# 128x128 turns in a two-layer hybrid decoder: one transposing matmul a block, or four 64x64 products on TensorE's four quarters

## The chip, the cores and the metric

The kernel runs on one core of one Trainium2 chip. The metric is the device time of one execution in microseconds (us). All matmuls run on TensorE, whose results land in PSUM banks of 128 partitions x 512 fp32 columns; ScalarE and VectorE copy them out.

## The reference

Two layers of a causal decoder trunk on x of shape (1, 256, 1024) in fp32, each with two half-step feed-forward blocks around four parallel mixers:

```python
x = x + 0.5 * swiglu(rmsnorm(x), w_gate, w_up, w_down)      # 1024 -> 2816 -> 1024
h = rmsnorm(x); parts = split(h @ w_in)                      # 1024 -> 12288
y = [hgrn2(q, f, i, g), s5(u), conformer_conv(a, b), dilated_attention(q, k, v)]   # each 512 wide
x = x + (sum(sigmoid(gate_k) * (y_k @ w_branch_k))) @ w_out
x = x + 0.5 * swiglu(rmsnorm(x), ...)
```

A last rmsnorm ends it. Attention has 12 heads of 128 (3 groups of dilation 1, 4 and 16) with partial rotary positions; the 256 tokens are two blocks of 128.

## The kernel before

The work is bound to weights that are read once. A stream (`Stream`) loads fp32 weights from HBM, ScalarE rounds them to a high part (`whi`) and VectorE takes the low part (`wlo`), both as fp32r; each product of activations and weights is three fp32r matmuls (`mm3`: high x high, high x low, low x high). The activations are split in the same way by `split`: one ScalarE copy and one VectorE subtraction, from PSUM or SBUF.

TensorE runs the products of one stage behind the other: `cols_tok` makes rows of tokens (512 columns a matmul), `cols_feat` and `rows_feat` make rows of features (256 columns, all tokens). The mixers' own work (rope and attention, HGRN2, S5, the convolution, the tables of S5) is written as generators in a list `side`; after each piece of a stage `tick` steps them, as far as `room` allows. It decides by clocks that a planner keeps for each engine (`Paced`), with costs such as `pe_cost` for TensorE. `finish` steps a job to its end without regard to the clocks, where its result is needed. PSUM has four accumulation banks and four others (`mx`), which side jobs reserve with `grab` and `drop` from the count `free`.

Between the stages tensors are turned, from tokens on partitions to features on partitions or back, in blocks of 128x128. Such a turn is `T.transpose(bank[:, ...], block, ident)`: the block is the stationary operand and the identity matrix the moving one. Four blocks fill one bank, which is then copied out:

- `norm_turn` (L913): the normed activations `xn` of one token block, 8 blocks in two banks `xT`, then split into `hTh` and `hTl`. `norm.turn(0)` stands among the last matmuls of the stage before; `norm.turn(1)` stands in the next stage between its matmuls for the first and the second 128 tokens.
- `turn` in `ffn` (L986): the first 512 columns of the gated activations, 4 blocks for each token block, `gT`.
- `s5_tables` (L632): tables `b4` (4 blocks in each of 4 banks a layer) and `s5c`.
- `rope_turn` (L1369): queries and keys, up to 4 heads for each token block, `rt`, copied out by heads.
- `attend` (L1416): the weights `scores` after the exponential, 3 blocks for the first 128 queries and 6 (in two banks one behind the other) for the others, `pTb`; copied to `pT`, which is the stationary operand of the product with the values (`apv`).
- `hgrn`, `conv` and the end of `attend`: the mixers' outputs, `yaT`, `cT` and `cB`, `ydT`, 4 blocks a bank.

The S5 mixer makes its small products as 64x64x64 matmuls on the four quarters of TensorE: rows 0 to 63 or 64 to 127 of the operands by partitions 0 to 63 or 64 to 127 of the result (names `s5k`, `yk`, `w`, `y`). `yk` goes through the quarters in the order (0, 0), (1, 1), (0, 1), (1, 0) of operand half and result half.

Of the kernel before, what the change touches and what calls it, by code (L numbers as in the profile page):

```python
# [75 lines left out]
def size(ap):  # L76
    return math.prod(ap.shape[1:])
# [29 lines left out]
def pe_cost(name, args):  # L107
    if name == "transpose":
        return 0.11
    n = size(args[2])  # L110
    return max(0.107, n / 2370 * (1 if args[2].dtype == FR else 4))
# [77 lines left out]
def trunk(ctx, tc, x_in, positions, ffn1_norm, ffn1_w_gate, ffn1_w_up, ffn1_w_down, mix_norm, w_in,  # L189
# [31 lines left out]
    def tiny(shape, name, bufs=4):  # L221
        return sb.tile(shape, F32, tag=name, name=name, bufs=bufs)

# [138 lines left out]
    free = [3]  # L362
# [269 lines left out]
    def s5_tables(l):  # L632
# [51 lines left out]
        for half in range(2):  # L684
            hs = slice(4 * half, 4 * half + 4)
            bv = [bb[:, k].rearrange("p (a h) c -> p a h c", a=2)[:, :, hs, None, :] for k in range(2)]
            qv = [pq[:, k].rearrange("p i (a h) -> p a h i", a=2)[:, :, hs, :, None] for k in range(2)]
            for k, op in ((0, ALU.subtract), (1, ALU.add)):
# [7 lines left out]
                yield  # L696
                b = mx_bank(f"b4{half}{k}")
                ov = o.rearrange("p h a i c -> p h (a i c)")
                for h in range(4):
                    T.transpose(b[:, h * P:(h + 1) * P], ov[:, h], ident)  # L700
                S.activation(B4[half][:, :, k, :], b.rearrange("p (h s) -> p h s", h=4), AF.Copy)
                yield GO
# [9 lines left out]
        for k in range(2):  # L712
            b = mx_bank(f"s5c{k}")
            for a in range(4):
                T.transpose(b[:, a * P:(a + 1) * P], craw[k][:, a].rearrange("p g s -> p (g s)"), ident)
            bv = b.rearrange("p (j g c) -> p j g c", g=2, c=16)
            for g in range(2):
                S.activation(ct[64 * g:64 * g + 64, k], bv[64 * g:64 * g + 64, :, g, :], AF.Copy)
            yield
# [193 lines left out]
    def norm_turn(t, xn, n, hT):  # L913
        for b in range(2):
            bank = tr_bank(f"xT{n}_{t}{b}")
            for i in range(4):
                f = 4 * b + i
                T.transpose(bank[:, i * P:(i + 1) * P], xn[:, f * P:(f + 1) * P], ident)
            bv = bank.rearrange("p (k f) -> p k f", k=4)
            split(hT[0][b][:, :, t * P:(t + 1) * P], hT[1][b][:, :, t * P:(t + 1) * P], bv)  # L920
# [46 lines left out]
    def ffn(norm, tail):  # L967
# [3 lines left out]
        for c, (c0, n) in enumerate(FFC):  # L971
# [5 lines left out]
            if c == 0:  # L977
# [4 lines left out]
                def ev_up(t, bank, gh=gh, gl=gl, sg=sg):  # L982
                    V.tensor_tensor(sg[t], bank, sg[t], op=ALU.mult)
                    g = sg[t]

                    def turn():  # L986
                        yield
                        b = tr_bank(f"gT{t}")
                        for i in range(4):
                            T.transpose(b[:, i * P:(i + 1) * P], g[:, i * P:(i + 1) * P], ident)  # L990
                        split(gh[:, :, t * P:(t + 1) * P], gl[:, :, t * P:(t + 1) * P],
                              b.rearrange("p (k f) -> p k f", k=4))
                    start(turn())
# [69 lines left out]
    def mixers(l, norm, tail, g_tab):  # L1063
# [7 lines left out]
        def pair(name):  # L1071
            return H([P, 4, 256], name + "h", FR), H([P, 4, 256], name + "l", FR)


        def hgrn():
# [103 lines left out]
            yT[0] = pair("yA")  # L1179
            for t in range(2):  # L1180
# [15 lines left out]
                y = H2([P, 512], "ya")  # L1196
# [6 lines left out]
                b2 = tr_bank(f"yaT{t}")  # L1203
                for i in range(4):
                    T.transpose(b2[:, i * P:(i + 1) * P], y[:, i * P:(i + 1) * P], ident)
                split(yT[0][0][:, :, t * P:(t + 1) * P], yT[0][1][:, :, t * P:(t + 1) * P],
                      b2.rearrange("p (k f) -> p k f", k=4))
                yield
# [107 lines left out]
        def conv():  # L1316
# [15 lines left out]
            for t in range(2):  # L1332
                yield from grab()
                b = tr_bank(f"cT{t}")
                for fb in range(4):
                    T.transpose(b[:, fb * P:(fb + 1) * P], a[:, fb, t * P:(t + 1) * P], ident)
                st = tiny([P, 6], "bst", 2)
                mv = tiny([P, 4], "bmv", 2)
                V.bn_stats(st, b)
# [5 lines left out]
                V.tensor_scalar(xc[t], b, mv[:, 0:1], mv[:, 3:4], op0=ALU.subtract, op1=ALU.mult)  # L1345
                drop()
                yield
            yT[2] = pair("yC")
            for half in range(2):
                b = tr_bank(f"cB{half}")  # L1350
                for i in range(2):
                    fb = 2 * half + i
                    for t in range(2):
                        T.transpose(b[:, i * 256 + t * P:i * 256 + (t + 1) * P], xc[t][:, fb * P:(fb + 1) * P], ident)
                y = H2([P, 2, 256], "yc")
                for i in range(2):
# [3 lines left out]
                    S.activation(y[:, i, :], b[:, i * 256:(i + 1) * 256], AF.Silu, bias=vcol[:, cb_:cb_ + 1],  # L1360
                                 scale=vcol[:, cg:cg + 1])
                split(yT[2][0][:, 2 * half:2 * half + 2, :], yT[2][1][:, 2 * half:2 * half + 2, :], y)
                yield
# [5 lines left out]
        def rope_turn(raw, pieces, name):  # L1369
# [14 lines left out]
            for t in range(2):  # L1384
                b = tr_bank(f"{name}{t}")
                for i in range(n):
                    T.transpose(b[:, i * P:(i + 1) * P], rv[:, t, i, :], ident)
# [290 lines left out]
```

## Time and profile before

| | |
|---|---|
| median of 3 runs | 1568.28 us (1562.89 to 1569.6) |
| profiled execution | 1563.96 us, span 1562.3 us |
| TensorE matmuls | busy 1548.3 us (99%), 11419 instructions |
| weight loads of TensorE | busy 1413.7 us (90%) |
| VectorE | busy 1104.7 us (71%) |
| ScalarE | busy 843.4 us (54%) |
| DMA | weight queue 51.9% of 16 engines' span, HBM 179 GB/s |
| granted TensorE clock | 0.997 of full speed |

Busy time counts an engine as busy while an instruction of it is in flight. Matmuls are pipelined: one lasts 218 to 400 ns, and the next starts long before it has ended, so what a matmul costs is the distance from its start to the next one's start. In the tables of rows PE is TensorE's matmul side, PEld its weight loads, DVE is VectorE, ACT ScalarE. L72 is the line of the planner's wrapper, through which nearly every instruction is issued, so groups are told apart by the names of their tiles.

### The profile page before, as it was taken

What the parts mean: (1) busy time and instruction counts of PE and PEld (TensorE: products, weight loads), DVE (VectorE), ACT (ScalarE), POOL (GpSimd) and SP (SyncE); (2) the same over time, 40 slices, a digit from 0 to 9 for tenths busy, and PEclk for the clock granted to TensorE, in tenths of its full rate; (3) what the DMA queues carried; (4) which work ended last, traced back from release to release, by engine and by line L of the source; (5) the groups of instructions that cost most, each with busy time, mean ns of one, the idle gap of its engine ahead of it and who ended that gap; (6) DMA issues with size and microseconds to landing.
All of it is one profiled execution on the core that took longest, in us unless ns stands there. A gap on an engine that the chain in (4) does not pass through costs nothing.

```text
span 1562.3 us, 27640 instructions
## 1 busy us (share of the span) xinstructions
PE 1548.3 (99%) x11419; PEld 1413.7 (90%) x11419; DVE 1104.7 (71%) x1767; ACT 843.4 (54%) x1212; POOL 28.0 (2%) x75
## 2 busy tenths in 40 slices
PE   9999999999999999999999999999999999999998
PEld 7999888889899998999889988988899999989986
DVE  6787676966878866555497766568869887665553
ACT  5644465666565465444354553656665565654442
POOL 2000000000000000000000000000000000000000
PEclk9999999999999999999999999999999999999999
DMA  7566556453544556556556564665345544645561
GB/s 274 189 194 218 189 182 202 153 172 109 162 163 162 177 183 220 189 183 214 183 176 197 188 216 160 205 197 167 129 137 170 180 163 163 227 164 191 196 217 58
DMA packets 179376, 281.94 MB, mean 180 GB/s; under 512 B 26703, under 2 KB 82065, under 8 KB 179250
## 3 DMA queue, kind: packets, MB, share of 16 engines
q1 hardware_dynamic: 154096, 270.03, 51.9%
q10 hardware_dynamic: 24834, 9.97, 2.6%
q8 instruction: 89, 1.46, 0.4%
q14 instruction: 37, 0.30, 0.1%
q0 software_dynamic: 320, 0.18, 0.0%
HBM read 277.01 MB, written 3.15 MB: 179 GB/s over the span
## 4 chain that ended last, share of the span: by engine, by line
PE 96%; ACT 1%; DVE 1%; issue 1%; DMA 1%; POOL 0%; ACTq 0%; SPq 0%; POOLq 0%; DVEq 0%
PE down L72 15%; PE gate_h L72 13%; PE up_h L72 13%; PE att_t L72 12%; PE pgt_h L72 11%; PE br L72 6%; PE gate_t L72 3%; PE up_t L72 3%; PE po_t L72 3%; PE pi_t L72 1%; PE pu_h L72 1%; PE pb_h L72 1%; PE pg_t L72 1%; PE pa_h L72 1%; PE glu L72 1%; PE pq_h L72 1%
## 5 line engine op out<-in xcount | busy, mean ns | idle before, releaser
L72 DVE TENSOR_TENSOR wlo<-raw,whi 128x1024 fp32r<-128x1024 f32 x512 | 614.4, 1220 | 185.7 <-ACT whi L72 88.4
L72 ACT ACTIVATE whi<-raw 128x1024 fp32r<-128x1024 f32 x512 | 526.6, 1055 | 157.6 <-PE down L72 90.1
L72 PE MATMUL gate_h<-hTh,whi 128*128 128x256 f32 x576 | 160.1, 278 | 0.0
L72 PE MATMUL up_h<-hTh,whi 128*128 128x256 f32 x576 | 159.3, 277 | 0.0
L72 PE MATMUL gate_h<-hTh,wlo 128*128 128x256 f32 x576 | 159.1, 276 | 0.0
L72 PE MATMUL gate_h<-hTl,whi 128*128 128x256 f32 x576 | 159.1, 276 | 0.0
L72 PE MATMUL up_h<-hTh,wlo 128*128 128x256 f32 x576 | 159.0, 276 | 0.0
L72 PE MATMUL up_h<-hTl,whi 128*128 128x256 f32 x576 | 159.0, 276 | 0.0
L72 PE MATMUL pgt_h<-hTh,whi 128*128 128x256 f32 x512 | 144.9, 283 | 0.0
L72 PE MATMUL pgt_h<-hTl,whi 128*128 128x256 f32 x512 | 141.9, 277 | 0.0
L72 PE MATMUL pgt_h<-hTh,wlo 128*128 128x256 f32 x512 | 141.9, 277 | 0.0
L72 PE MATMUL down<-whi,gl 128*128 128x512 f32 x352 | 138.5, 393 | 0.0
L72 PE MATMUL down<-whi,gh 128*128 128x512 f32 x352 | 138.1, 392 | 0.0
L72 PE MATMUL down<-wlo,gh 128*128 128x512 f32 x352 | 138.0, 392 | 0.0
L72 PE MATMUL att_t<-whi,hTh 128*128 128x512 f32 x288 | 118.6, 412 | 0.0
L72 PE MATMUL att_t<-whi,hTl 128*128 128x512 f32 x288 | 114.3, 397 | 0.0
L72 PE MATMUL att_t<-wlo,hTh 128*128 128x512 f32 x288 | 113.6, 395 | 0.0
L72 PEld LDWEIGHTS gate_h<-hTl,whi 128*128 128x128 f32 x576 | 108.2, 188 | 0.0
L72 PEld LDWEIGHTS gate_h<-hTh,whi 128*128 128x128 f32 x576 | 108.2, 188 | 0.1
L72 PEld LDWEIGHTS up_h<-hTl,whi 128*128 128x128 f32 x576 | 108.1, 188 | 0.0
L72 PEld LDWEIGHTS up_h<-hTh,whi 128*128 128x128 f32 x576 | 108.1, 188 | 0.0
L72 PEld LDWEIGHTS gate_h<-hTh,wlo 128*128 128x128 f32 x576 | 108.1, 188 | 0.0
(391 smaller groups left out, 3344.8 us busy)
## 6 DMA issues: line engine op xcount, KB each, us to landing
raw<-in_w_in_dram SPq DMA_DIRECT2D x60, 1024.0 KB, 5.2
raw<-in_ffn_w_up_dram SPq DMA_DIRECT2D x44, 1024.0 KB, 5.3
raw<-in_ffn_w_down_dram SPq DMA_DIRECT2D x44, 1024.0 KB, 4.9
raw<-in_ffn_w_gate_dram SPq DMA_DIRECT2D x42, 1024.0 KB, 5.1
raw<-in_w_in_dram SPq DMA_DIRECT2D x72, 512.0 KB, 4.6
raw<-in_w_branch_dram SPq DMA_DIRECT2D x16, 1024.0 KB, 5.0
raw<-in_w_out_dram SPq DMA_DIRECT2D x8, 1024.0 KB, 5.1
raw<-in_s_w_glu_dram SPq DMA_DIRECT2D x16, 256.0 KB, 3.8
```

Of the source, the lines that this page charges most:

```text
L72: return f(*args, **kw)
```

## The change

Each turn becomes four plain matmuls of 64x64 blocks with the matching 64x64 corner of the identity matrix, one on each quarter of TensorE. A helper `turn` takes a list of up to eight 128x128 blocks and fills two banks: bank `r` holds, for each block, the 64 columns that come from its rows 64r to 64r + 63. What was two groups of four blocks, one for each token block or each half, becomes one call of eight where both are there: `gT`, `rt`, `yaT` and `ydT` (by `turn_out`), `b4`, `s5c`, `cB`; attention turns its six blocks at once before the product with the values. The copies out of PSUM read a bank with 64 tokens of each block, and write them to their place (`half_rows`); for `norm_turn` these are four copies of 256 columns in place of two of 512. Side jobs reserve two banks for a turn, and `free` goes from 3 to 4. The planner's `pe_cost` has a price of 0.036 us for a matmul whose stationary operand is 64x64, which holds for the S5 products too (0.108 us before).

```diff
--- before.py
+++ after.py
@@ -108,6 +108,8 @@
     if name == "transpose":
         return 0.11
     n = size(args[2])
+    if args[1].shape[0] == 64 and size(args[1]) == 64:
+        return 0.036
     return max(0.107, n / 2370 * (1 if args[2].dtype == FR else 4))
 
 
@@ -220,6 +222,20 @@
 
     def tiny(shape, name, bufs=4):
         return sb.tile(shape, F32, tag=name, name=name, bufs=bufs)
+
+    def turn(name, blocks):
+
+
+        banks = [mx_bank(f"{name}{r}") for r in range(2)]
+        for i, src in enumerate(blocks):
+            for r, c in ((0, 0), (1, 1), (0, 1), (1, 0)):
+                rs, cs = slice(64 * r, 64 * r + 64), slice(64 * c, 64 * c + 64)
+                T.matmul(banks[r][cs, 64 * i:64 * i + 64], src[rs, cs], ident[rs, rs], start=True, stop=True)
+        return banks
+
+    def half_rows(ap, r, pattern):
+
+        return ap.rearrange(pattern + " (t r q) -> " + pattern + " t r q", r=2, q=64)[..., r, :]
 
     def split(hi, lo, src, eng_hi=None):
         S.activation(hi, src, AF.Copy)
@@ -359,7 +375,7 @@
             for j in list(side):
                 step(j)
 
-    free = [3]
+    free = [4]
 
     def grab(n=1):
 
...
@@ -693,13 +710,13 @@
                     V.tensor_tensor(u2[:, :, a], bv[1 - k][:, a].to_broadcast([P, 4, 4, 16]),
                                     qv[1][:, a].to_broadcast([P, 4, 4, 16]), op=ALU.mult)
                 V.tensor_tensor(o, u1, u2, op=op)
-                yield
-                b = mx_bank(f"b4{half}{k}")
-                ov = o.rearrange("p h a i c -> p h (a i c)")
-                for h in range(4):
-                    T.transpose(b[:, h * P:(h + 1) * P], ov[:, h], ident)
-                S.activation(B4[half][:, :, k, :], b.rearrange("p (h s) -> p h s", h=4), AF.Copy)
-                yield GO
+                ov.append(o.rearrange("p h a i c -> p h (a i c)"))
+                yield GO if k == 0 else None
+            banks = turn(f"b4{half}", [o[:, h] for o in ov for h in range(4)])
+            for r in range(2):
+                S.activation(B4[half][:, :, :, 64 * r:64 * r + 64].rearrange("p h k q -> p k h q"),
+                             banks[r].rearrange("p (k h q) -> p k h q", k=2, h=4), AF.Copy)
+            yield GO
         dx = H2([16, 2, 4, 16], "dx")
         V.tensor_copy(dx, draw[:, :, None, :].to_broadcast([16, 2, 4, 16]))
         yield
@@ -709,14 +726,14 @@
         V.tensor_copy(dcol, b[:, 0:16])
 
         ct = H2([P, 2, 16, 16], "ct")
-        for k in range(2):
-            b = mx_bank(f"s5c{k}")
-            for a in range(4):
-                T.transpose(b[:, a * P:(a + 1) * P], craw[k][:, a].rearrange("p g s -> p (g s)"), ident)
-            bv = b.rearrange("p (j g c) -> p j g c", g=2, c=16)
+        banks = turn("s5c", [craw[k][:, a].rearrange("p g s -> p (g s)") for k in range(2) for a in range(4)])
+        for r in range(2):
+            bv = banks[r].rearrange("p (a j g c) -> p a j g c", j=2, g=2, c=16)
+            cv = ct.rearrange("p k (a r j) c -> p (k a) r j c", r=2, j=2)
             for g in range(2):
-                S.activation(ct[64 * g:64 * g + 64, k], bv[64 * g:64 * g + 64, :, g, :], AF.Copy)
-            yield
+                gs = slice(64 * g, 64 * g + 64)
+                S.activation(cv[gs, :, r], bv[gs, :, :, g, :], AF.Copy)
+        yield
         for half in range(2):
             hs = slice(8 * half, 8 * half + 8)
             cv = [ct[:, k, hs, None, :].to_broadcast([P, 8, 4, 16]) for k in range(2)]
@@ -911,13 +928,12 @@
     norm_no = [0]
 
     def norm_turn(t, xn, n, hT):
+        banks = turn(f"xT{n}_{t}", [xn[:, f * P:(f + 1) * P] for f in range(8)])
         for b in range(2):
-            bank = tr_bank(f"xT{n}_{t}{b}")
-            for i in range(4):
-                f = 4 * b + i
-                T.transpose(bank[:, i * P:(i + 1) * P], xn[:, f * P:(f + 1) * P], ident)
-            bv = bank.rearrange("p (k f) -> p k f", k=4)
-            split(hT[0][b][:, :, t * P:(t + 1) * P], hT[1][b][:, :, t * P:(t + 1) * P], bv)
+            for r in range(2):
+                ts = slice(t * P + 64 * r, t * P + 64 * r + 64)
+                split(hT[0][b][:, :, ts], hT[1][b][:, :, ts],
+                      banks[r][:, 256 * b:256 * b + 256].rearrange("p (k q) -> p k q", k=4))
 
     class Norm:
 
@@ -981,16 +997,15 @@
 
                 def ev_up(t, bank, gh=gh, gl=gl, sg=sg):
                     V.tensor_tensor(sg[t], bank, sg[t], op=ALU.mult)
-                    g = sg[t]
-
-                    def turn():
+
+                    def turn_g():
                         yield
-                        b = tr_bank(f"gT{t}")
-                        for i in range(4):
-                            T.transpose(b[:, i * P:(i + 1) * P], g[:, i * P:(i + 1) * P], ident)
-                        split(gh[:, :, t * P:(t + 1) * P], gl[:, :, t * P:(t + 1) * P],
-                              b.rearrange("p (k f) -> p k f", k=4))
-                    start(turn())
+                        banks = turn("gT", [sg[t][:, i * P:(i + 1) * P] for t in range(2) for i in range(4)])
+                        for r in range(2):
+                            split(half_rows(gh, r, "p i"), half_rows(gl, r, "p i"),
+                                  banks[r].rearrange("p (t i q) -> p i t q", t=2, i=4))
+                    if t == 1:
+                        start(turn_g())
                 cols_tok(hT, ev_gate, "gate0", outer=True, between=lambda: norm.turn(1), at=3 if norm.n == 0 else 4,
                          mid=norm.n == 0)
                 cols_tok(hT, ev_up, "up0")
@@ -1071,6 +1086,17 @@
         def pair(name):
             return H([P, 4, 256], name + "h", FR), H([P, 4, 256], name + "l", FR)
 
+        def turn_out(b, y):
+
+            yT[b] = pair("y" + "ABCD"[b])
+            yield from grab(2)
+            banks = turn(f"y{b}T", [y[t][:, i * P:(i + 1) * P] for t in range(2) for i in range(4)])
+            for r in range(2):
+                split(half_rows(yT[b][0], r, "p i"), half_rows(yT[b][1], r, "p i"),
+                      banks[r].rearrange("p (t i q) -> p i t q", t=2, i=4))
+            drop(2)
+            yield
+
 
         def hgrn():
             qT, kT, Pm = m["qT"], m["kT"], m["lf"]
...
@@ -1193,19 +1219,14 @@
                 V.tensor_scalar(ss[:, 0:4], ss[:, 0:4], EPS, None, op0=ALU.add)
                 G.tensor_tensor(ss[:, 4:8], ss[:, 0:4], neghalf.to_broadcast([P, 4]), op=ALU.pow)
                 yield
-                y = H2([P, 512], "ya")
+                ys[t] = y = H2([P, 512], "ya")
                 for h in range(4):
                     hs = slice(h * P, (h + 1) * P)
                     V.scalar_tensor_tensor(y[:, hs], b[:, hs], ss[:, 4 + h:5 + h], sgn[:, t, hs], op0=ALU.mult,
                                            op1=ALU.mult)
                 drop()
                 yield
-                b2 = tr_bank(f"yaT{t}")
-                for i in range(4):
-                    T.transpose(b2[:, i * P:(i + 1) * P], y[:, i * P:(i + 1) * P], ident)
-                split(yT[0][0][:, :, t * P:(t + 1) * P], yT[0][1][:, :, t * P:(t + 1) * P],
-                      b2.rearrange("p (k f) -> p k f", k=4))
-                yield
+            yield from turn_out(0, ys)
 
 
         def s5():
@@ -1330,36 +1351,38 @@
             yield
             xc = {}
             for t in range(2):
-                yield from grab()
-                b = tr_bank(f"cT{t}")
-                for fb in range(4):
-                    T.transpose(b[:, fb * P:(fb + 1) * P], a[:, fb, t * P:(t + 1) * P], ident)
-                st = tiny([P, 6], "bst", 2)
+                yield from grab(2)
+                banks = turn(f"cT{t}", [a[:, fb, t * P:(t + 1) * P] for fb in range(4)])
+                st = tiny([P, 2, 6], "bst", 2)
                 mv = tiny([P, 4], "bmv", 2)
-                V.bn_stats(st, b)
+                for r in range(2):
+                    V.bn_stats(st[:, r], banks[r][:, 0:256])
                 V.bn_aggr(mv[:, 0:2], st)
                 V.tensor_scalar(mv[:, 2:3], mv[:, 1:2], EPS, None, op0=ALU.add)
                 G.tensor_tensor(mv[:, 3:4], mv[:, 2:3], neghalf, op=ALU.pow)
                 yield
                 xc[t] = H2([P, 512], f"xc{t}")
-                V.tensor_scalar(xc[t], b, mv[:, 0:1], mv[:, 3:4], op0=ALU.subtract, op1=ALU.mult)
-                drop()
+                for r in range(2):
+                    V.tensor_scalar(half_rows(xc[t], r, "p"), banks[r][:, 0:256].rearrange("p (b q) -> p b q", b=4),
+                                    mv[:, 0:1], mv[:, 3:4], op0=ALU.subtract, op1=ALU.mult)
+                drop(2)
                 yield
             yT[2] = pair("yC")
+            yield from grab(2)
+            banks = turn("cB", [xc[t][:, fb * P:(fb + 1) * P] for fb in range(4) for t in range(2)])
             for half in range(2):
-                b = tr_bank(f"cB{half}")
-                for i in range(2):
-                    fb = 2 * half + i
-                    for t in range(2):
-                        T.transpose(b[:, i * 256 + t * P:i * 256 + (t + 1) * P], xc[t][:, fb * P:(fb + 1) * P], ident)
                 y = H2([P, 2, 256], "yc")
                 for i in range(2):
                     fb = 2 * half + i
                     cg = col["lg"] + 4 * l + fb
                     cb_ = col["lbn"] + 4 * l + fb
-                    S.activation(y[:, i, :], b[:, i * 256:(i + 1) * 256], AF.Silu, bias=vcol[:, cb_:cb_ + 1],
-                                 scale=vcol[:, cg:cg + 1])
+                    for r in range(2):
+                        S.activation(half_rows(y[:, i, :], r, "p"),
+                                     banks[r][:, fb * P:(fb + 1) * P].rearrange("p (t q) -> p t q", t=2), AF.Silu,
+                                     bias=vcol[:, cb_:cb_ + 1], scale=vcol[:, cg:cg + 1])
                 split(yT[2][0][:, 2 * half:2 * half + 2, :], yT[2][1][:, 2 * half:2 * half + 2, :], y)
+                if half == 1:
+                    drop(2)
                 yield
 
 
@@ -1381,13 +1404,13 @@
             V.tensor_tensor(A, xa, cb, op=ALU.mult)
             V.tensor_tensor(xa, A, B, op=ALU.add)
             yield
-            for t in range(2):
-                b = tr_bank(f"{name}{t}")
-                for i in range(n):
-                    T.transpose(b[:, i * P:(i + 1) * P], rv[:, t, i, :], ident)
-                bv = b[:, :n * P].rearrange("p (a e q) -> p a e q", e=2, q=P)
-                for a, e, h, k, g, m_ in by_head(pieces):
-                    S.activation(att[k, h][:, g:g + m_, t * P:(t + 1) * P], bv[:, a:a + m_, e, :], AF.Copy)
+            yield from grab(2)
+            banks = turn(name, [rv[:, t, i, :] for t in range(2) for i in range(n)])
+            for a, e, h, k, g, m_ in by_head(pieces):
+                for r in range(2):
+                    bv = banks[r][:, :n * P].rearrange("p (t a e q) -> p a e t q", t=2, e=2, q=64)
+                    S.activation(half_rows(att[k, h], r, "p g")[:, g:g + m_], bv[:, a:a + m_, e], AF.Copy)
+            drop(2)
             yield
 
         def ev_att(ci):
@@ -1456,35 +1479,26 @@
                 yield
 
                 blocks = [(g, kb) for g in range(3) for kb in range(qb + 1)]
+                n = len(blocks)
+                yield from grab(2)
+                banks = turn("pTb", [sc[:, g, kb * P:(kb + 1) * P] for g, kb in blocks])
+                pT = (H if qb else H2)([P, n, P], "pT")
+                for r in range(2):
+                    S.activation(half_rows(pT, r, "p a")[:, :, 0], banks[r][:, :64 * n].rearrange("p (a q) -> p a q", q=64),
+                                 AF.Copy)
+                drop(2)
+                yield
                 yield from grab()
                 bo = mx_bank("apv")
-
-                def pv(i0, part, pT):
-                    for i, (g, kb) in enumerate(part):
-                        T.matmul(bo[:, 0:P], pT[:, i, :], v[:, kb, g * P:(g + 1) * P],
-                                 start=(i0 + i == 0), stop=(i0 + i == len(blocks) - 1))
-                for i0 in range(0, len(blocks), 3):
-                    part = blocks[i0:i0 + 3]
-                    b = tr_bank("pTb")
-                    for i, (g, kb) in enumerate(part):
-                        T.transpose(b[:, i * P:(i + 1) * P], sc[:, g, kb * P:(kb + 1) * P], ident)
-                    pT = H2([P, 3, P], "pT")
-                    S.activation(pT, b[:, :384].rearrange("p (a q) -> p a q", a=3), AF.Copy)
-                    yield
-                    pv(i0, part, pT)
+                for i, (g, kb) in enumerate(blocks):
+                    T.matmul(bo[:, 0:P], pT[:, i, :], v[:, kb, g * P:(g + 1) * P], start=(i == 0), stop=(i == n - 1))
+                yield
                 V.tensor_scalar(yd[qb][:, h * P:(h + 1) * P], bo[:, 0:P], sm[:, 1:2], None, op0=ALU.mult)
                 drop()
                 yield
             if h < 3:
                 return
-            yT[3] = pair("yD")
-            for t in range(2):
-                b = tr_bank("ydT")
-                for i in range(4):
-                    T.transpose(b[:, i * P:(i + 1) * P], yd[t][:, i * P:(i + 1) * P], ident)
-                split(yT[3][0][:, :, t * P:(t + 1) * P], yT[3][1][:, :, t * P:(t + 1) * P],
-                      b.rearrange("p (k f) -> p k f", k=4))
-                yield
+            yield from turn_out(3, yd)
 
 
         def ev_i(t, bank):
```

## Rows read from the trace of the kernel before

**Rows 1.** The profile's page: busy time by engine, and the chain that ended last.
```profile
PE 1548.3 (99%) x11419; PEld 1413.7 (90%) x11419; DVE 1104.7 (71%) x1767; ACT 843.4 (54%) x1212; POOL 28.0 (2%) x75
...
PE 96%; ACT 1%; DVE 1%; issue 1%; DMA 1%; POOL 0%; ACTq 0%; SPq 0%; POOLq 0%; DVEq 0%
```
**Rows 2.** The chain in order of time: start us, us, engine, line, tile, count.
```profile
49.07 10.88 PE up_h L72 x96
...
174.85 22.68 PE down L72 x99
```
**Rows 3.** TensorE's groups by shape: count, busy us, mean ns, idle before.
```profile
L72 PE MATMUL xT<-ident,xn 128*128 128x128 f32 x96 | 14.1, 288 | 0.2
L72 PE MATMUL rt<-ident,rq 128*128 128x128 f32 x96 | 13.4, 276 | 0.9 <-ACT ak L72 0.9
L72 PE MATMUL pTb<-ident,scores 128*128 128x128 f32 x72 | 11.8, 272 | 0.0
...
L72 PE MATMUL b<-ident,b 128*128 128x128 f32 x32 | 4.8, 272 | 0.0
...
L72 PE MATMUL ydT<-ident,yd 128*128 128x128 f32 x16 | 2.4, 272 | 0.0
```
**Rows 4.** TensorE's timeline around eight turns of rope: start us, us, instruction, count.
```profile
352.24 1.03 PE L72 MATMUL rt<-ident,rq 128*128 128x128 f32 x8
353.03 0.36 PE L72 MATMUL pb_h<-hTh,whi 128*128 128x256 f32 x1
353.23 0.28 PE L72 MATMUL pb_h<-hTl,whi 128*128 128x256 f32 x1
```
**Rows 5.** TensorE's groups by shape: one group of the S5 products.
```profile
L72 PE MATMUL w<-U,B 64*64 64x64 f32 x256 | 4.6, 221 | 0.0
```
**Rows 6.** TensorE's timeline around 32 instructions on the quarters.
```profile
217.34 0.28 PE L72 MATMUL pu_h<-hTh,wlo 128*128 128x256 f32 x1
217.55 0.69 PE L72 MATMUL s5k<-CA,BA 64*64 64x64 f32 x32
218.17 0.38 PE L72 MATMUL pu_h<-hTh,whi 128*128 128x256 f32 x1
218.39 0.28 PE L72 MATMUL pu_h<-hTl,whi 128*128 128x256 f32 x1
```
**Rows 7.** TensorE's timeline around 64 instructions on the quarters.
```profile
259.11 0.40 PE L72 MATMUL pg_t<-whi,hTl 128*128 128x512 f32 x1
259.44 1.16 PE L72 MATMUL yk<-U,K 64*64 64x64 f32 x64
260.53 0.50 PE L72 MATMUL pg_t<-whi,hTh 128*128 128x512 f32 x1
260.86 0.39 PE L72 MATMUL pg_t<-wlo,hTh 128*128 128x512 f32 x1
```
**Rows 8.** Waits of the weight loader: total us, times, longest us.
```profile
PEld hl L72 <- DVE KL L72: 4.0, 2, 2.1
...
PEld gate_t L72 <- DVE hTl L72: 2.1, 6, 0.4
...
PEld w L72 <- issue: 1.4, 4, 0.4
```
**Rows 9.** ScalarE's groups by shape: two reads of PSUM.
```profile
L72 ACT ACTIVATE hTh<-xT 128x512 fp32r<-128x512 f32 x24 | 13.3, 595 | 2.8 <-PE xT L72 2.4
...
L72 ACT ACTIVATE glus<-glu 128x256 f32<-128x256 f32 x8 | 3.1, 384 | 1.3 <-PE glu L72 1.1
```
**Rows 10.** Timeline of the weight loader in the second turn before the mixers.
```profile
206.64 0.42 PEld L72 LDWEIGHTS xT<-ident,xn 128*128 128x128 f32 x4 [0.24 <-PE xT L72]
207.32 0.19 PEld L72 LDWEIGHTS pi_t<-whi,hTh 128*128 128x128 f32 x1 [0.26 <-ACT hTh L72]
```
**Rows 11.** Instructions of the tile ydT: ns min/median/max, first and last start us.
```profile
L72 PE MATMUL ydT<-ident,yd x16: 270/272/273, 512.3 to 1288.2; 128*128 128x128 f32 x16
```
**Rows 12.** Instructions of the tile yDh: the branch product that reads it.
```profile
L72 PE MATMUL br<-yDh,whi x64: 276/276/276, 532.7 to 1314.3; 128*128 128x256 f32 x64
```

More of the change, by code (lines that the diff above doesn't have):

```diff
@@ L687, in s5_tables @@
             qv = [pq[:, k].rearrange("p i (a h) -> p a h i", a=2)[:, :, hs, :, None] for k in range(2)]
+            ov = []
             for k, op in ((0, ALU.subtract), (1, ALU.add)):
@@ L1178, in hgrn @@
             v, sgn = m.pop("v"), m.pop("sg")
-            yT[0] = pair("yA")
+            ys = {}
             for t in range(2):
```

## Prediction

> **What bounds the kernel now.** I read the profile's busy shares and the chain of waits first. TensorE is busy 99% of the 1562.3 us span, and the chain that ended last lies 96% on it [rows 1]. A busy matmul engine need not be at its pace, so the next view was the chain in order of time: 96 matmuls with 256 columns take 10.88 us, 0.1133 us a step, and 99 with 512 columns 22.68 us, 0.229 us a step [rows 2]. These steps are the same from one stage to the next, so nothing slows TensorE inside its long runs: time put on it or taken off it moves the end one for one. VectorE (71%) and ScalarE (54%) have room, and only count where TensorE waits for them.
>
> **What the turns cost now.** The groups of matmuls by shape show each 128x128 turn as one matmul instruction with `ident` as the moving operand [rows 3]. Five groups stand there: xT 96, rt 96, pTb 72, b 32, ydT 16. gT is like b (32), and cB, s5c, cT and yaT are like ydT (16 each), so 408 turns in all. Their price on TensorE's line is in the timeline [rows 4]: eight turns start at 352.24, and the second matmul behind them starts at 353.23. Less one step of 0.1133 that is 0.877 us, 0.110 us a turn; 408 make 44.7 us.
>
> **What takes their place.** A plain fp32 product is two instructions in this trace: `s5` makes 2 layers x 2 halves x 32 = 128 products of 64x64x64 into `w`, and the group counts 256 matmuls [rows 5]. A turn as a matmul has two operands, data and `ident`, both fp32, so it will be two instructions as well: 408 x 4 x 2 = 3264 in place of 408. The matmul count goes from 11419 [rows 1] to 14275. The kernel already runs such products on the four quarters, so their price is in the trace. One run of 32 instructions stretches two 256-column steps from 217.34 to 218.39 [rows 6]: 1.05 - 2 x 0.1133 = 0.82 us. A run of 64, in the very order of quarters that `turn` has, stretches two 512-column steps from 259.11 to 260.86 [rows 7]: 1.75 - 2 x 0.229 = 1.29 us. Two runs make a line: 0.47 / 32 = 0.0147 us an instruction, and 0.35 us for each run whatever its length. The 0.35 shows elsewhere too: the loader of weights idles 1.4 us in 4 entries into `w`, put down to issue [rows 8].
>
> Of this the Trainium skill has a rule: its page TensorEngine Tiling (Array Packing), section Key Properties, says that a change of tiling mode drains the engine. The trace agrees, with 0.35 us a run. Without a drain the 3264 instructions would cost 48.0 us, and the change 3 us; with it, it costs what follows.
>
> **The sum on TensorE.** The diff makes 62 runs: 38 of eight blocks (xT 12, rt 10, gT, b4 4 each, cB, s5c, yA, yD 2 each), 8 of six and 8 of three (the two query blocks of attention), 8 of four (rt 4, cT 4); 304 + 48 + 24 + 32 = 408 blocks. So 3264 x 0.0147 = 48.0, and 62 x 0.35 = 21.7, together 69.7 us, less 44.7 that go: **+25.0 us**. An eight-block turn costs 1.29 for 0.88 us. Merging groups saves nothing on this engine, as 0.877 already holds a group's entry and exit. Bounds: if half of the 0.35 hides behind waits that TensorE has anyway, +14 us; if every instruction costs what the short run gives as a whole, 0.82 / 32 = 0.0256 us, 83.6 us, +39 us.
>
> **Evacuations.** Most keep their count: gT, yA, yD, B4, ct and rope read two banks before and after, in pieces of 64 tokens. `norm_turn` goes from two copies of 512 columns (595 ns each) for a token block to four of 256 (384 ns by the nearest read of 256 PSUM columns) [rows 9], about 4 us more on ScalarE over 12 turns and about as much on VectorE; both have idle time for it, except in `norm.turn(1)`, six times, where TensorE has nothing else to do. There the second four turns load at 206.64 and the next product starts at 207.32 [rows 10]; 0.68 us, since the first four were copied meanwhile. After the change the first copy can begin only when all eight blocks are through, and the product needs both row halves: 0.47 (32 instructions) + 0.22 (one instruction's length [rows 5]) + 2 x 0.384 = 1.46 us, 0.78 later. Of it 0.41 is in the sum already. The rest, 6 x 0.37 = 2.2 us, is the upper bound; nothing is the lower, as today's later wait for `hTl` (2.1 us over 6 entries into gate_t [rows 8]) falls into the same time. I take +1 us. Bank norm in halves and twice as many small Silu pieces stand behind VectorE's and ScalarE's slack; uncovered they would be a few tenths each.
>
> **The planner.** `pe_cost` lowers each 64x64 product from 0.108 to 0.036 us, so the planner's TensorE clock runs 2.3 us less ahead in each run of 32 `s5` products, where the trace had 1.29 us and the planner 3.5. Side jobs will come out a little later, which can end waits such as the 4.0 us of `hl` for `KL` [rows 8] or make as many new ones: -4 to +4 us, taken as 0. The fourth `free` bank and `grab(2)` swap waits on TensorE for waits in the planner, which cost nothing while the jobs have slack: `ydT` is turned at 512.3 [rows 11], and the first branch product that needs it starts at 532.7 [rows 12].
>
> **Forecast.** The profiled execution took 1563.96 us around its 1562.3 us span; + 25.0 + 1 = 1590. The three runs shown have a median of 1568.28, 4.3 above it, and go from 1562.89 to 1569.6; I put the forecast at **1591 us**, and one half per cent, 7.8 us, is about what a measurement can tell from no change.
>
> **Rivals.**
> *Late side jobs.* Each turn now grabs two of four banks, `s5` holds two and `hgrn` one for long, and attention's `pT` of six blocks takes a heap tile. If rope, attention or conv fall more than their slack behind (20 us by rows 11 and 12), `finish` empties them without pacing, and TensorE waits through copies and exponentials. Against it: the waits for such jobs are 4 us at most today. With the long side of the instruction price it is 1604 us. Chance 0.15.
> *One instruction a product.* If a product with `ident` came out as one instruction, as a turn does now, an eight-block turn would cost what the 32-instruction run does, 0.82 for 0.88 us: 1632 x 0.0147 + 21.7 = 45.7, +1, and with the evacuations 1566 us: no change. Against it: every fp32 product in the trace is two. Chance 0.06. The same end (+3, 1568) comes if the 0.35 us is not paid at all: 0.03.
> *The quarters really at once* (the other side). If the four quarters streamed independently, a pass would cost 64 of the 256 columns of a 0.1133 us step, 0.028 us, and four of them would share it: 0.0071 us an instruction, and the next run would start while the last drains. 3264 x 0.0071 = 23 us, 22 less than now: 1542 us. It decides once an eight-block turn costs under 0.75 us. The Trainium skill's page TensorE: Matmul & The Clock Gate, section Measured speedup vs the span model, lets packed tiles start some 4 ns apart, which speaks for it. Against it stand the runs of this trace, 64 instructions in 1.29 us in just this order. Chance 0.04.
>
> The forecast itself holds 0.72. Together: slower by over 0.5% 0.87, within 0.09, faster 0.04. The range, 1576 to 1606 us, goes from half of the run's fixed part hidden (+14, less 2) to the dear end of the instruction price (+39, and 3 for waits); the cases below it hold 0.13.
>
> **What the profile after would show.** 14275 matmuls; runs `xT`, `rt`, `gT` as 64*64 forms of 64 instructions, some 1.1 us from first start to the next full product and 1.29 us with both late steps; the loader idle on issue some 0.35 us at 62 more entries; the long runs still at 0.1133 and 0.229 us a step; ScalarE's `hTh` 48 times at about 0.38 us. If the 64*64 forms count 1632, the second rival holds; if eight blocks pass in under 0.75 us, the third; if TensorE's idle time grows by over 8 us with ACT or DVE as releaser, the first. The prediction fails if a product by `ident` runs at another pace than products by data, which no row here can show.

## The result, and the profile after

The changed kernel takes 1588.64 us (1586.61 to 1590.93, 4 runs), where 1591 was forecast, against 1566.88 us before, a ratio of 1.015 with a 95% interval of 1.013 to 1.017: 21.8 us slower, where the sum of the forecast has 26. The profiled execution has a span of 1585.9 us, 23.6 more than before.

The page of the changed kernel, busy time by engine (against [rows 1]):
```profile
PE 1564.4 (99%) x14275; PEld 1422.7 (90%) x14275; DVE 1108.7 (70%) x1799; ACT 842.0 (53%) x1247; POOL 30.0 (2%) x75
```
The count is the forecast one, and TensorE is as full as before. Its groups by shape (against [rows 3] and [rows 5]):
```profile
L72 PE MATMUL xT<-ident,xn 64*64 64x64 f32 x768 | 15.1, 230 | 0.0
L72 PE MATMUL rt<-ident,rq 64*64 64x64 f32 x768 | 15.1, 222 | 3.8 <-issue 2.4 <-ACT ak L72 1.4
L72 PE MATMUL pTb<-ident,scores 64*64 64x64 f32 x576 | 12.0, 223 | 0.0
...
L72 PE MATMUL gT<-ident,sg 64*64 64x64 f32 x256 | 4.6, 221 | 0.0
```
768 is 96 x 4 x 2: each product is two instructions. Nothing in these rows looks dear: xT is busy for 15.1 us and was for 14.1. Busy time unites what overlaps; the cost is in the distance between starts. TensorE's timeline around the first gT turn, start us and us first (against [rows 4] and [rows 7]):
```profile
43.79 0.28 PE L72 MATMUL gate_h<-hTh,wlo 128*128 128x256 f32 x1
44.00 1.16 PE L72 MATMUL gT<-ident,sg 64*64 64x64 f32 x64
45.09 0.38 PE L72 MATMUL gate_h<-hTh,whi 128*128 128x256 f32 x1
45.31 0.29 PE L72 MATMUL gate_h<-hTl,whi 128*128 128x256 f32 x1
```
From 43.79 to 45.31 are 1.52 us, less two steps of 0.1133 that is 1.29 us for eight blocks, to the hundredth what `yk` cost before. The chain in order of time shows the long stretches at the step of [rows 2]:
```profile
52.17 10.88 PE up_h L72 x96
63.05 10.88 PE gate_h L72 x96
```
What is new stands in TensorE's waits (total us, times, longest), where before only `hl` (3.2), the start (1.4), `rt` (0.9) and `gate_t` (0.8) stood:
```profile
PE gate_t L72 <- ACT hTh L72: 4.1, 4, 1.8
PE rt L72 <- issue: 2.4, 2, 1.2
PE gate_t L72 <- DVE wlo L72: 2.0, 2, 1.7
PE pi_t L72 <- ACT hTh L72: 1.5, 2, 0.8
```
The wait for `KL` in front of `hl` is gone, and the product behind a turn of the norm waits for `hTh`, 5.6 us in 6 entries: behind the second turn of five norms, and behind the first turn of the first norm, at the start of the kernel. ScalarE makes these copies as expected (against [rows 9]):
```profile
L72 ACT ACTIVATE hTh<-xT 128x256 fp32r<-128x256 f32 x48 | 16.5, 383 | 16.5 <-PE xT L72 10.3 <-DVE hTl L72 6.2
```

### The profile page after: what moved, and what is told of

Read it like the earlier page. It is cut to its first block, busy times and chain, and to the rows that moved or that the text cites. A ratio compares the mean times of both kernels' runs of the same rounds, so it can differ in the third digit from the quotient of the medians.

```text
span 1585.9 us, 33436 instructions
## 1 busy us (share of the span) xinstructions
PE 1564.4 (99%) x14275; PEld 1422.7 (90%) x14275; DVE 1108.7 (70%) x1799; ACT 842.0 (53%) x1247; POOL 30.0 (2%) x75
## 4 chain that ended last, share of the span: by engine, by line
PE 94%; ACT 2%; DVE 1%; issue 1%; DMA 1%; ACTq 0%; POOL 0%; SPq 0%; POOLq 0%; DVEq 0%
PE down L72 15%; PE gate_h L72 12%; PE up_h L72 12%; PE pgt_h L72 11%; PE att_t L72 10%; PE br L72 6%; PE po_t L72 3%; PE up_t L72 3%; PE gate_t L72 3%; PE pa_h L72 1%; PE pi_t L72 1%; PE pg_t L72 1%; PE pf_h L72 1%; PE glu L72 1%; PE pu_h L72 1%; PE pq_h L72 1%
```

## The experiments

Eleven kernels ran, on three chips; each ratio is against executions of the kernel before that were made with them, and these spread from 1561.5 to 1575.9 us. To compare the profiles I took the starts of all matmuls from each timeline. Of each long matmul, 0.1133 us (256 columns) or 0.229 us (512 columns) is its own step; what the steps between neighbouring long matmuls have beyond that, summed, is called *pace*, and all other time (turns, small products, waits) but some 3 us at the ends of the span *rest*. Both are in us of the one profiled execution and good to about 1 us; "stretches" is the duration of one matmul in the stretch behind the gT group of each of the four feed-forward blocks. The need for the column "pace" only came up in the second experiment; for e14 the two columns were not worked out.

| kernel | median us | ratio to before, interval | rest | pace | stretches, ns |
|---|---|---|---|---|---|
| before | 1566.88 | | 151.8 | 3.1 | 276 276 276 276 |
| changed | 1588.64 | 1.015 (1.013 to 1.017) | 173.5 | 5.0 | 276 276 276 276 |
| e1, price alone | 1568.32 | 1.0014 (0.9995 to 1.0033) | 150.2 | 14.0 | 276 281 276 281 |
| e5, all but the quarters | 1583.2 | 1.0114 (1.0094 to 1.0134) | 148.7 | 25.0 | 281 281 281 281 |
| e4, norm as before | 1580.75 | 1.0096 (1.0076 to 1.0115) | 165.1 | 6.7 | 276 276 276 276 |
| e3, broken runs | 1603.01 | 1.0239 (1.0214 to 1.0264) | 189.3 | 4.9 | 276 276 276 276 |
| e2, products twice | 1650.56 | 1.0509 (1.0465 to 1.0553) | 238.9 | 4.7 | 276 276 276 276 |
| e8, e5 with gT on quarters | 1570.28 | 1.0017 (0.9998 to 1.0036) | 151.1 | 9.8 | 276 276 276 276 |
| e11, e5 with a ninth turn | 1581.27 | 1.0068 (1.0043 to 1.0092) | 149.2 | 22.9 | 281 276 281 281 |
| e10, before with gT in one group | 1586.83 | 1.0103 (1.0077 to 1.0128) | 157.9 | 19.9 | 281 281 281 281 |
| e12, e5 ending on a quarter | 1578.69 | 1.0059 (1.0036 to 1.0081) | 149.9 | 23.0 | 276 281 281 281 |
| e13, e5 ending on a plain product | 1568.35 | 0.9995 (0.9978 to 1.0012) | 149.9 | 10.0 | 276 276 276 276 |
| e14, more such ends | 1566.36 | 0.9996 (0.9979 to 1.0013) | | | 276 276 276 276 |

**e1, the planner's price alone.** The kernel before, with
```diff
     n = size(args[2])
+    if args[1].shape[0] == 64 and size(args[1]) == 64:
+        return 0.036
```


> The kernel before with one line of the change alone: the planner's price of 0.036 us for a 64x64 product, which here touches the S5 products only. Theory (the time lies in TensorE's own work for the turns): TensorE has the same instructions as before, only the order of side jobs moves; ratio to before 0.997 to 1.003. Rival (the repriced planner makes waits that are a part of the slowdown): ratio 1.004 or more.


1568.32 us, and an interval that holds 1: the planner's part is nothing that can be measured. Its profiled execution, at a span of 1571.6, was 9 us longer than that of before, all of it in the column "pace".

**e5, everything but the quarters.** Each block turned by one transposing matmul, eight in two banks, copied out bank by bank; all else of the change stays:
```diff
-                T.matmul(banks[r][cs, 64 * i:64 * i + 64], src[rs, cs], ident[rs, rs], start=True, stop=True)
+            T.transpose(banks[i // per][:, P * (i % per):P * (i % per) + P], src, ident)
```


> Everything of the change except the quarters: the same calls of up to eight blocks, two banks grabbed, four free, the planner's price, six blocks of attention at once, but each block as one 128x128 transposing matmul, copied out bank by bank as before. Theory (the price is the products on the quarters): the whole 22 us go, 1560 to 1570 us, ratio to before 0.996 to 1.002. Rival (grabbing two banks and turning both token halves together delays side jobs and makes waits): 1575 us or more, ratio over 1.005.


1583.2 us: only 5 us came back, which looks like the rival's case. The waits don't show it: TensorE's idle time is no longer than with the quarters. The group of one main matmul does, in e5:
```profile
L72 PE MATMUL gate_h<-hTl,whi 128*128 128x256 f32 x576 | 161.8, 281 | 0.0
```
The same group in the changed kernel:
```profile
L72 PE MATMUL gate_h<-hTl,whi 128*128 128x256 f32 x576 | 159.1, 276 | 0.0
```
The same 576 matmuls, same shape, same operands, each 281 ns in place of 276. The chain of e5 shows what it does to the step:
```profile
1434.34 11.31 PE gate_h L72 x96
1445.65 11.31 PE up_h L72 x96
```
11.31 us for 96 is 0.1178 us a step, 4.5 ns more than [rows 2]; the feed-forward blocks have 6 x 576 = 3456 such matmuls, at most 15.5 us, and the other stretches at that step make the 25. The granted clock is 0.998 in e5 and 0.999 in the changed kernel, and 1.00 in these stretches in both, so it is not the clock. In the first block of e5 the step changes at the gT group: 0.113 before it and 0.118 behind it, up to the next interruption; in the third it is 0.118 ahead of the group already. At equal pace e5 stands 3.1 us *below* the kernel before (148.7 against 151.8), and the quarters cost 173.5 - 148.7 = 24.8 us.

**e4, the norm's turns as before.** `norm_turn` alone is that of the kernel before, with two banks of four transposing matmuls:
```diff
     def norm_turn(t, xn, n, hT):
-        banks = turn(f"xT{n}_{t}", [xn[:, f * P:(f + 1) * P] for f in range(8)])
...
+                T.transpose(bank[:, i * P:(i + 1) * P], xn[:, f * P:(f + 1) * P], ident)
```


> The changed kernel with the turns of the normed activations as before (12 of 62 turns: transposing matmuls, two copies of 512 columns). Theory: 12 x 0.41 = 5 us of TensorE's work go, and with them the longer waits for hTh behind the second turn (5.6 us in the changed trace, 0.8 us before), so 8 to 10 us less than the changed kernel: 1579 to 1581 us, ratio to before 1.008 to 1.010. Rival (these waits would be there anyway): 5 us less, 1584 us. Rival (the cost is elsewhere): no difference, 1589 us.


1580.75 us, as the theory said, and its waits for `hTh` are short again:
```profile
PE gate_t L72 <- ACT hTh L72: 1.0, 3, 0.4
```
The rest falls by 8.4 us: 12 x 0.41 = 4.9 of TensorE's work and 3.5 of waits. These are not all the norm's: at its twelve turns the rest falls by 7.2 us, and the 2.4 us of `rt` on issue are missing from e4's waits, though its turns are the same there.

**e3, runs broken in the middle.**
```diff
         for i, src in enumerate(blocks):
+            if i == 4:
+                T.transpose(banks[0][:, 256:384], src, ident)
```


> The changed kernel with one more 128x128 transposing matmul in the middle of each turn of more than four blocks (46 turns), into columns that the turn overwrites. Theory (each change between the quarters and the whole array costs 0.35 us): 46 x (0.11 + 0.35) = 21 us more than the changed kernel, about 1610 us, ratio to before 1.027 to 1.030. Rival (no price for the change of mode, only for instructions): 46 x 0.11 = 5 us, about 1594 us, ratio 1.018.


1603.01 us, 14.4 more than the changed kernel, between the two. The rest grows by 15.8 us, 0.34 for each of 46 breaks, but this is not the price of a break, since waits shrink at the same time: those listed for TensorE sum to 9.7 us in e3 and to 14.5 in the changed kernel. The price is in the timeline, here of the first gT turn with its break (65 counts the 64 and the transposing matmul):
```profile
42.90 0.28 PE L72 MATMUL gate_h<-hTh,wlo 128*128 128x256 f32 x1
43.10 1.58 PE L72 MATMUL gT<-ident,sg 64*64 64x64 f32 x65
44.62 0.39 PE L72 MATMUL gate_h<-hTh,whi 128*128 128x256 f32 x1
44.84 0.28 PE L72 MATMUL gate_h<-hTl,whi 128*128 128x256 f32 x1
```
From 42.90 to 44.84 are 1.94 us, against 1.52 without the break, and the other broken turns amid long matmuls have the same 0.42 us more. Less 0.11 for the matmul, a change to the whole array and back costs 0.31 us in the middle of a run, close to the theory's 0.35.

**e2, every product twice.** `for _ in range(2):` ahead of the product in `turn`.


> The changed kernel with each 64x64 product of a turn made twice, the second over the first: 3264 instructions more, no change of mode more. Theory (0.0147 us an instruction, 0.35 us a run): 48 us more than the changed kernel, 1637 us, ratio to before 1.043 to 1.047. Rival (an instruction costs 0.0256 us, as the short run gives as a whole): 84 us more, 1672 us, ratio 1.067.


1650.56 us in two executions, 62 more than the changed kernel by the medians and 56 by the ratios, nearer to the theory than to the rival, and above it. A run of 128 in its timeline, against the 1.16 us of 64 in the changed kernel:
```profile
44.95 2.24 PE L72 MATMUL gT<-ident,sg 64*64 64x64 f32 x128
```
1.08 / 64 = 0.0169 us for each added instruction, a repeat on the same quarter, against 0.0147 in the run as it was. 3264 of these are 55 us. Of what is left, waits are a part, one inside the dense runs of `rt` and one of a side job:
```profile
PE rt L72 <- issue: 3.6, 2, 2.6
PE hd L72 <- DVE E L72: 3.3, 2, 3.0
```

**e10, gT in one group of eight.** The kernel before, with the two groups of four put together behind the second token block, still transposing:
```diff
-                        b = tr_bank(f"gT{t}")
+                        bs = [tr_bank(f"gT{u}") for u in range(2)]
...
-                    start(turn())
+                    if t == 1:
+                        start(turn())
```


> The kernel before with one thing changed: gT turned in one group of eight transposing matmuls behind the second token block, in place of two groups of four. Theory (one group of eight in that place sets the slow pace for the feed-forward stretches behind it): 11.31 us for 96 matmuls in these, 1578 to 1583 us, ratio to before 1.008 to 1.011. Rival (the place is of no matter, another part of the change slows the stretches): 1566 us, ratio 0.998 to 1.002.


1586.83 us: this alone makes the kernel before nearly as slow as the whole change does (1588.64 us; the ratios, 1.0103 against 1.015, lie further apart than the medians), with no turn on the quarters. Its stretch:
```profile
658.70 11.31 PE gate_h L72 x96
```
16.8 us of it are pace. The other 6 are rest; waits that this order of jobs makes are a part, such as
```profile
PE s5k L72 <- ACT BA L72: 3.6, 2, 3.4
```

**e8, gT on the quarters again.** e5, with `turn` of the changed kernel for the four gT groups alone.


> The run with everything but the quarters, with the four gT turns alone on the quarters again. In that run the long stretches of the feed-forward blocks went at 11.31 us for 96 matmuls from the gT group on, against 10.88 in the changed kernel. Theory (the pace of a stretch is set by how the interruption before it ends, and has nothing to do with the work added): the stretches go at 10.88 again, some 15 to 18 us less, +1.6 us for four turns on the quarters: 1566 to 1570 us, ratio to before 1.000 to 1.003. Rival (the calls of eight blocks and the banks cost the time): 1585 us, ratio 1.012.


1570.28 us. 13 us go by making TensorE's work for these four turns dearer (rest + 2.4 us). With e10 this shows that gT's group sets the pace of up to 100 us behind it, and that e5's loss was no wait for banks or side jobs.

**e11, e12 and e13, what ends the group.** e5, with one instruction more behind the eight of gT, each writing the values over that are already there:
```diff
+ e11: T.transpose(banks[0][:, 0:P], sg[0][:, 0:P], ident)
+ e12: T.matmul(banks[0][0:64, 0:64], sg[0][0:64, 0:64], ident[0:64, 0:64], start=True, stop=True)
+ e13: T.matmul(banks[0][:, 0:P], sg[0][:, 0:P], ident, start=True, stop=True)
```


> The run with everything but the quarters, with the first block of gT turned once more at the end of each of the four gT groups: nine transposing matmuls for eight, 0.4 us of work more in all. Theory (the pace of a stretch is set by the instructions that end the interruption before it, odd or even): some 15 us less, 1566 to 1570 us. Rival (a group of transposing matmuls always sets the slow pace): 1583 us as without it, ratio 1.011.

> The run with everything but the quarters, and behind the eight transposing matmuls of each of the four gT groups one 64x64 product on one quarter, which writes the same values over a corner. Theory (what TensorE runs last before a stretch sets its pace, and an end on a quarter sets the quick one): 10.88 us for 96 matmuls in the feed-forward stretches, 13 to 15 us less than without the product, 4 x 0.38 us more: 1568 to 1572 us, ratio to before 1.001 to 1.004. Rival (the copies out of the banks, by row halves, set it): 1584 us, ratio 1.011.

> The same with one plain 128x128 product in place of the one on a quarter. Theory (an end on a quarter sets the quick pace, since the change of mode empties the engine): the slow pace stays, 11.31 us for 96, 1584 us, ratio 1.011. Rival (any other instruction at the end will do): 1568 to 1572 us.


1581.27, 1578.69 and 1568.35 us: all three theories fell. A ninth turn, odd for even, brought one block of four, the second, to the step of 0.1133. An end on a quarter brought one of four, the first; the matmuls of e12 in the first and in the second feed-forward block:
```profile
L72 PE MATMUL gate_h<-hTh,whi x84: 276/276/276, 60.0 to 109.9; 128*128 128x256 f32 x84
```
```profile
L72 PE MATMUL gate_h<-hTh,whi x79: 281/281/281, 654.8 to 704.9; 128*128 128x256 f32 x79
```
Within a stretch minimum, median and maximum are one number: the pace is taken up at the interruption and kept. One plain 128x128 product at the end brought all four blocks to 276 ns, the time that the theory had given to its rival; that any other instruction will do, as the rival said, does not hold in e11 and e12.
```profile
L72 PE MATMUL gate_h<-hTl,whi 128*128 128x256 f32 x576 | 159.1, 276 | 0.0
```
So e13 is everything of the change but the quarters, at the shorter step in these blocks, and it takes as long as the kernel before (ratio 0.9995): what is left up to the changed kernel's 1.015 is the price of the quarters in whole executions, with no need of the two columns.

**e14, such ends at more groups.** The same product in `turn` for gT, cB, b4 and s5c.
```diff
+        if name[:2] in ("gT", "cB", "b4", "s5"):
+            T.matmul(banks[0][:, 0:P], blocks[0], ident, start=True, stop=True)
```


> The run with everything but the quarters, with one plain 128x128 product at the end of each gT, cB, b4 and s5c group (12 groups). Theory (such an end sets the quick pace in the stretch behind it): beside the feed-forward stretches those behind cB and the tables go quick too, some 4 us less than with the product at gT alone, 0.3 us a product more: 1563 to 1567 us, ratio to before 0.996 to 0.999, a version a little better than both. Rival (the end that works at gT does not work elsewhere): 1568 to 1571 us.


1566.36 us, no difference from before that can be measured. The stretch behind cB did go at 276 ns (e13 has 281 in this group):
```profile
L72 PE MATMUL br<-yCl,whi 128*128 128x256 f32 x64 | 17.7, 276 | 0.0
```
What that gains over e13 is 2 us by the medians, half of what was expected, and nothing by the ratios; no version here beats the kernel before.

## Why the prediction was right

**TensorE's work for the turns** was the step that carried it: +25.0 us, and +1 for the norm's waits. The timelines have every kind of run at the price of the sum where no wait falls into it: eight blocks 1.29 to 1.30 us, six 1.06, four 0.83 and three 0.72, against 0.89 for eight, 0.45 for four and 0.34 for three before. Over all groups that is 70.0 us in place of 44.8, **+25.2**. The drain rule behind it holds nearly as it stands: e3 has 0.31 us for a change in the middle of a run, where the step took 0.35 for each run. At equal pace the quarters cost 24.8 us net of all waits (changed against e5). With e4 the norm's 12 turns are 8.4 of these, so the other 50 cost 16.4 us where the sum has 20.0; as the runs have their price, the difference is in waits, and e5 has some that e4 lacks, such as 2.5 us of `rt` for `yk`.

**The norm's waits** came out near their size, +1 us taken and 2.2 the bound. Against e4, five of the six exposed turns take 0.66 to 0.74 us more, 0.41 of it work: 1.4 us of waits. The sixth, the first turn of the kernel, has the longest entry of that wait, 1.8 us, but about 1 us of it is not the turn's: ScalarE rounds the first weights (`whi`) before it copies this turn, and here they landed late. The rounding starts at 9.31 us, in the other twelve traces between 6.5 and 8.5.
```profile
9.31 1.06 ACT L72 ACTIVATE whi<-raw 128x1024 fp32r<-128x1024 f32 x1 [4.17 <-DMA raw<-in_ffn_w_gate_dram]
10.27 0.64 ACT L72 ACTIVATE hTh<-xT 128x256 fp32r<-128x256 f32 x2
```
In e3, where it starts at 7.36 us, the same wait is 0.8 us.

**The planner, the banks, the order** were taken as 0 with bounds of 4 us either way. The planner's price alone is 1.0014, and everything but the quarters, at equal pace, comes out 3.1 us below the kernel before. That brings the 24.8 down to 21.7 of rest, and with 1.9 of pace the profiled execution is 23.6 us longer. The rival of late side jobs is ruled out as the cause by the same number. That the whole lies so near the sum is in part luck: TensorE's listed waits grew by 8.2 us, from 6.3 to 14.5, of which the sum had 1, and smaller delays around turns and between long matmuls, which the waits do not list, must have shrunk by 11.7 (25.2 + 8.2 + 1.9 less 23.6).

**One instruction a product** and **quarters really at once** are refuted by the count, 14275, and by 1.29 us an eight-block turn, far from the 0.75 that the latter needs. The page TensorE: Matmul & The Clock Gate of the Trainium skill, section Measured speedup vs the span model, with starts some 4 ns apart, describes these runs only in part: four instructions, two products, start 6 to 7 ns apart, but then 38 ns pass to the next four, which makes 14.7 ns in the mean.

**"Nothing slows TensorE inside its long runs"** was nearly true of both kernels compared (3.1 and 5.0 us of pace), but as a premise it was luckier than it looked. Shorter stretches at 0.1178 us stand in both, such as 71 matmuls of `pgt_h` from 437.0 us on before. Both kernels happen to have the step of 0.1133 us behind gT in all four feed-forward blocks. Had the change merged the gT groups and kept the transposing matmuls, as e5 and e10 do, 15 us would have come from a place that the sum held constant.

**The profile's signs.** The loader's wait on issue was to show at 62 more entries; the waits list it at some 25 (`rt` 10, `xT` 8, `pTb` 6, `b` 1), so it is a sign of a change of mode and no count of them. Two of `rt`'s entries are of another kind: 1.2 us in the middle of a run of 64, behind 26 and 34 of its instructions, with another dense run of 64 (`rt` or `y`) right ahead of it.

## What to carry to other kernels

Price a small-tile product by a run of the same length from the trace, start to start, with the late steps at both ends; busy time and mean durations hid the price here, and a turn by plain products is eight instructions a block where a transposing matmul is one. When one part of a change is undone and the time does not come back, compare the durations of the untouched instructions before looking for a new wait: 276 against 281 ns, four times a kernel, hid 20 us here. And a difference of two totals is no price where waits change as well: by the totals a break of e3 costs 0.34 us, in the timeline 0.42.

## What the runs showed of the hardware

The same stream of weight load and 256-column matmul goes at one of two steps, 0.1133 or 0.1178 us, for up to 100 us at a time, at granted clocks of 0.996 to 0.999. It changes only where another kind of instruction comes between. Which of them it takes up is open. In the feed-forward blocks an end on a plain 128x128 product gave the shorter step in 8 of 8 (e13, e14), a run on the quarters the shorter one in all blocks of the five kernels that have it there, eight transposing matmuls the longer one in 8 of 8 (e5, e10), two groups of four the shorter in all of the kernel before but in two of four of e1, which has the same instructions there. So the ending alone does not decide it, and in the changed kernel a run of 64 for `s5c` is followed by 155 matmuls at the longer step. The choice also seems to differ between executions of one kernel, which one profile each cannot show: the twelve executions of e1 lie at 1562.6 to 1563.0 us (2), 1567.8 to 1568.6 (6) and 1573.3 to 1573.7 (4), and the profiled one, with two blocks at the longer step and 10.9 us more pace than before, is of the last group. Timing against other engines was not tried.

A second surprise is TensorE waiting on issue inside dense runs, 2.4 us in the changed kernel and 3.6 at `rt` with the products doubled, which runs of 64 amid long matmuls do not show.
